# Cache rows, queries and new keys and values on SyncE's DMA queue instead of GpSimd's

## The chip, the cores and the metric

The kernel runs on one core of a Trainium2 chip. A core has five engines with an instruction stream each: TensorE (PE; its weight loads are listed apart as PEld), VectorE (DVE), ScalarE (ACT), GpSimd (POOL) and SyncE (SP). An engine that issues a DMA puts it on a queue of its own; 16 DMA engines move the bytes of all queues. The metric is the device time of one launch in microseconds, as the median of several runs.

## The reference

One layer of a decoder is computed for a prompt group (256 tokens) and a sample group (8 sequences of 4 new tokens with 1024 cached ones), all in float32. What matters here is its attention branch. There are three groups of 4 heads with 128 dimensions, and group (window, dilation) attends to every dilation-th key back to the window's end:

```python
DIL_GROUPS = ((128, 1), (512, 4), (2048, 16))
h = _rms_norm(x, g_pre_mix)
(qa, ka, va, za, ba, aa, qb, kb, vb, uc, ga, gb, gc) = _split(h @ w_in, IN_SPLITS)
...
def _dilated_group(q, k, v, q_idx, dil, n_back):
    dist = jnp.arange(n_back + 1) * dil
    idx = q_idx[:, None] - dist[None, :]
    ...
    kg = k[:, idx].astype(jnp.float32)
    vg = v[:, idx].astype(jnp.float32)
    s = jnp.einsum('bqhd,bqjhd->bqhj', q.astype(jnp.float32), kg) * (HD_B ** -0.5)
    s = jnp.where(valid[None, :, None, :], s, -jnp.inf)
    m = jnp.max(s, axis=-1)
    p = jnp.exp(s - m[..., None])
    return jnp.einsum('bqhj,bqjhd->bqhd', p, vg), m, jnp.sum(p, axis=-1)
...
    else:
        kv_all = [jnp.concatenate([win_hists[gi].astype(dt), kv_new[gi]], axis=1) for gi in range(N_GROUPS)]
        q_idxs = [kv.shape[1] - T + jnp.arange(T) for kv in kv_all]
        ob = _dilated_mixture([qb[:, :, gi] for gi in range(N_GROUPS)],
                              [kv[:, :, 0] for kv in kv_all], [kv[:, :, 1] for kv in kv_all], q_idxs)
    win_new = [kv_all[gi][:, -win:] for gi, (win, _) in enumerate(DIL_GROUPS)]
```

`_dilated_mixture` joins the three groups by their softmax denominators. Beside this branch there are a gated delta rule and a pooling branch, three gated projections that merge them, and a SwiGLU. Outputs are the activations and the new caches; the attention's caches (`win1` to `win3`, for prompt and sample) hold the new keys and values.

## The kernel before, in words

All 288 tokens (256 prompt, 32 sample) are worked on together, and what sets the time is the stream of weights: 585 tiles `raw` of 128 x 1024 float32 (512 KB), loaded by SyncE at L169 into five buffers. ScalarE casts each to `wh` (L180), VectorE takes the rest `wl` (L184), and TensorE does 24 matmuls with them (L253 to L255: high by high, low by high, high by low). Later a few more DMAs (L165) copy old cache rows to the outputs.

Beside this stream run background jobs, each a Python generator that emits its next instructions as tiles are taken, at so many a tile; `paced` ties these to the last `wl`, so that VectorE's order is tiles and background work interleaved. `attn_sample` is the one for the sample group, with 4.4 instructions of VectorE a tile (`R_S`). Its data:

- `nat`: the new queries, keys and values, transposed on TensorE (`knat`, L973) and brought to SBUF by ScalarE (L979) and VectorE (L981). From there the prompt's keys and values go to the output (`win_prompt`, L986, 128 KB each), and the sample's go to a DRAM scratch `scr` (L988, 32 KB) and to the output (`win_sample`, L991, 32 KB). `nat` shares its buffers (`U`) with other tensors, `oah` (L146) among them.
- `qt` and `big`: queries spread over partitions, from `scr` (L1089, L1095).
- `kr`: a cache row for 128 combinations, 128 x 512 float32 (256 KB), in five buffers (`KR`). A pass over keys (VectorE, L1142) and a pass over values (L1190, L1192) use 48 rows each of groups 2 and 3 (L1106), 8 each of group 1 (L1111), and a few from `scr` (L1089, L1112).

The sources of L1106 and L1111 differ in their leading indices. For L1106 it is four neighbouring cache rows, and then 32 combinations of sequence and query; for L1111 it is 128 combinations at once:

```python
for g, dil, n in ((1, 4, 32), (2, 16, 16)):
    src = cw[g].rearrange("b (q m r) k h d -> m k r (b q) (h d)", q=4, r=dil)
    ... dq.dma_start(kr, src[m, kv][:4])
src = cw[0].rearrange("b (s m) k h d -> m k (b s) (h d)", m=8)
    ... dq.dma_start(kr, src[m, kv])
```

A row four ahead is asked for before the row that VectorE works on next. A DMA in an engine's stream stands there until its buffer is free, and what the same engine issues later stands behind it. Prompt attention (`pv`, L1065, and `sc`, L1042 to L1057) runs on TensorE, ScalarE and VectorE in the same part of the program.

Of the kernel before, what the change touches and what calls it, by code (L numbers as in the profile page):

```python
# [17 lines left out]
NT, NP, NS = 288, 256, 32  # L18
# [6 lines left out]
KR = 5  # L25
EPS = 1e-6
SC = 128.0 ** -0.5
WIN = (128, 512, 1028)
# [60 lines left out]
class Layer:  # L89
# [865 lines left out]
    def evac_qkv(self, kind, g):  # L955
        vT = []

        def evac(h, ps):
            nc = self.nc
            t = self.res.popleft()  # L960
            nc.scalar.copy(t, ps)
            if kind == 2:
                vT.append(t)
            else:
                (self.kT if kind == 1 else self.qT)[g, h] = t
            if h < 3:
                return
            src = vT if kind == 2 else [(self.kT if kind == 1 else self.qT)[g, j] for j in range(4)]
            for tb in ([2] if kind == 0 else [1, 2] if (kind == 1 and g == 0) else [0, 1, 2]):
                w = NS if tb == 2 else 128  # L970
                p = self.ps("knat")
                for j in range(4):
                    nc.tensor.transpose(p[:w, j * 128:j * 128 + 128], src[j][:, tb * 128:tb * 128 + w],  # L973
                                        self.c["ident"])
                for hp in range(2):
                    n = self.U(name="nat")
                    cs = slice(hp * 256, hp * 256 + 256)
                    if hp == 0:
                        nc.scalar.copy(n[:w, :256], p[:w, cs])  # L979
                    else:  # L980
                        nc.vector.tensor_copy(n[:w, :256], p[:w, cs])  # L981
                    if tb < 2:
                        if not (g == 0 and tb == 0):
                            o = self.o[f"win{g + 1}_prompt"][0, 0].rearrange("r k h d -> r k (h d)")
                            r0 = 0 if g == 0 else tb * 128
                            self.dq.dma_start(o[r0:r0 + 128, kind - 1, cs], n[:, :256])  # L986
                    else:
                        self.dq.dma_start(self.scr[kind, g][:, cs], n[:NS, :256])  # L988
                        if kind > 0:
                            o = self.o[f"win{g + 1}_sample"][0].rearrange("b r k h d -> b r k (h d)")  # L990
                            self.dq.dma_start(o[:, WIN[g] - 4:, kind - 1, cs], n[:NS, :256])  # L991
                    if kind == 2 and tb < 2:
                        self.vn[g, tb, hp] = n
                    else:
                        self.free(n)
            self.free(*vT)
        evac.res = 4
        return evac
# [78 lines left out]
    def attn_sample(self, pool):  # L1077
        nc, c, a, scr = self.nc, self.c, self.a, self.scr
        dq = nc.gpsimd
        qt = pool.tile([128, 2, 512], F32, name="qt")  # L1080
        big = pool.tile([128, 4, 512], F32, name="big")
# [4 lines left out]
        def by_t(dst, kind, g):  # L1086
            src = scr[kind, g].rearrange("(b t) d -> t b d", t=4)
            for t in range(4):
                dq.dma_start(dst[t * 32:t * 32 + 32], src[t][:, None, :].to_broadcast([8, 4, 512]))  # L1089

        for g in (1, 2):
            by_t(qt[:, g - 1], 0, g)
        q0s = scr[0, 0].rearrange("(b t) d -> t b d", t=4)
        for t in range(4):
            dq.dma_start(big[:, t], q0s[t][:, None, :].to_broadcast([8, 16, 512]))  # L1095
        cw = [a["cache_win1"][0], a["cache_win2"][0], a["cache_win3"][0]]

        def row():
# [2 lines left out]
        def sources(kv):  # L1101

            for g, dil, n in ((1, 4, 32), (2, 16, 16)):
                src = cw[g].rearrange("b (q m r) k h d -> m k r (b q) (h d)", q=4, r=dil)
                for m in range(n):
                    yield g, (m if g == 1 else 32 + m), lambda kr, s=src[m, kv][:4]: dq.dma_start(kr, s)  # L1106
            for g in (1, 2):
                yield g, 47 + g, lambda kr, g=g: by_t(kr, 1 + kv, g)
            src = cw[0].rearrange("b (s m) k h d -> m k (b s) (h d)", m=8)
            for m in range(8):  # L1110
                yield 0, m, lambda kr, s=src[m, kv]: dq.dma_start(kr, s)  # L1111
            yield 0, 8, lambda kr: dq.dma_start(kr, scr[1 + kv, 0][:, None, :].to_broadcast([32, 4, 512]))  # L1112

        todo = deque((kv,) + r for kv in range(2) for r in sources(kv))
        got = deque()

        def load():
            kv, g, m, fill = todo.popleft()
            kr = row()
            fill(kr)  # L1120
            got.append((kv, g, m, kr))
# [7 lines left out]
                if not got:  # L1129
                    return  # L1130

        for _ in range(KR - 1):
            load()
        yield 5

# [44 lines left out]
        for g, m, kr in rows(1):  # L1180
            for h in range(4):
                hs = slice(h * 128, h * 128 + 128)
                for t in (range(4) if g == 0 else (0,)):
                    dst = o0[:, t, hs] if g == 0 else ot[:, hs]
# [336 lines left out]
```

## Time and profile before

| | |
|---|---|
| median of 3 runs | 2061.14 us (2057.72 to 2062.92) |
| the profiled execution | 2068.37 us, span 2066.6 us, mean granted clock 0.992 |
| busy | TensorE 2010.6, VectorE 1324.2, ScalarE 893.8, GpSimd 291.6 us |
| bytes on SyncE's queue (q1, hardware) | 384.72 MB |
| bytes on GpSimd's queue (q0, software) | 37.73 MB |
| keys' pass of `attn_sample` on VectorE | 452.3 to 742.9 us |
| values' pass | 775.9 to 1051.3 us |

Times are of one profiled execution. An engine's busy time is the sum of its instructions without waits. In a row of waits the engine and its instruction come first, then what it waited for, the sum in us, how often, and the longest; in a row of one line's DMAs stand count, issue time in ns (least, median, most) and the times of the first and the last. "Landing" is the time from a DMA's issue to its completion. The DMA share is the mean busy share of the 16 DMA engines, where an engine with packets of two queues at once counts for both.

### The profile page before, as it was taken

The page shows a single profiled execution, that of the slowest core. Times are in us where ns is not written, and L with a number is a line of the kernel's source. Part 1 is how long each engine was busy: PE and PEld are TensorE (multiplying, and loading weights), DVE is VectorE, ACT ScalarE, POOL GpSimd, SP SyncE. Part 2 cuts the span into 40 slices and gives each one's busy share as a digit, 9 for nine tenths or more (in the row PEclk, how much of TensorE's full clock was granted, in tenths as well). Part 3 has the DMA queues.
Part 4 walks back from the last instruction along what each step waited for, and adds up shares of the span by engine and source line. Part 5 has one row for each costly group of instructions (what it writes and reads, how often), then busy time and mean ns, then how long its engine had stood idle before and what let it go on. Part 6 is the DMA issues. An engine that isn't in the chain of part 4 may idle for free. (4 is left out here: it accounts for less than half of the span.)

```text
span 2066.6 us, 38707 instructions
## 1 busy us (share of the span) xinstructions
PE 2010.6 (97%) x15212; PEld 1984.4 (96%) x15212; DVE 1324.2 (64%) x2857; ACT 893.8 (43%) x1414; POOL 291.6 (14%) x504
## 2 busy tenths in 40 slices
PE   8999999999799999989999989999999999999998
PEld 8989998999799999989999989999999999999997
DVE  7969558567688779878875475543554445454555
ACT  6654473453344444333334454334333333333344
POOL 2326312523320022322000000000000000000001
PEclk9999999999999999999999989999999999999999
DMA  8565546959995668998677646766767767677662
GB/s 268 160 182 169 176 140 197 228 173 238 219 205 183 181 184 198 226 220 245 195 229 234 218 160 212 226 222 217 225 216 228 230 217 226 218 225 227 217 205 97
DMA packets 240310, 425.50 MB, mean 206 GB/s; under 512 B 42736, under 2 KB 83200, under 8 KB 238464
## 3 DMA queue, kind: packets, MB, share of 16 engines
q1 hardware_dynamic: 207712, 384.72, 63.1%
q0 software_dynamic: 32272, 37.73, 8.0%
q8 instruction: 119, 1.95, 0.4%
q10 hardware_dynamic: 144, 0.59, 0.1%
q14 instruction: 63, 0.52, 0.1%
HBM read 410.44 MB, written 66.63 MB: 231 GB/s over the span
## 5 line engine op out<-in xcount | busy, mean ns | idle before, releaser
L184 DVE TENSOR_TENSOR wl<-raw,wh 128x1024 fp32r<-128x1024 f32 x585 | 720.2, 1232 | 519.0 <-ACT wh L180 516.7
L180 ACT CAST wh<-raw 128x1024 fp32r<-128x1024 f32 x585 | 612.7, 1050 | 917.9 <-PE m L254 792.3
L253 PE MATMUL m<-hh,wh 128*128 128x288 f32 x1792 | 532.7, 299 | 4.2 <-ACT wh L180 3.7
L255 PE MATMUL m<-hh,wl 128*128 128x288 f32 x1792 | 524.0, 298 | 8.3 <-DVE wl L184 8.3
L254 PE MATMUL m<-hl,wh 128*128 128x288 f32 x1792 | 531.3, 298 | 0.0
L253 PE MATMUL m<-xgh,wh 128*128 128x288 f32 x1408 | 415.8, 297 | 4.0 <-ACT xgh L373 4.0
L254 PE MATMUL m<-xgl,wh 128*128 128x288 f32 x1408 | 415.8, 296 | 3.2 <-DVE xgl L374 3.2
L255 PE MATMUL m<-xgh,wl 128*128 128x288 f32 x1408 | 414.6, 296 | 0.0
L255 PEld LDWEIGHTS m<-hh,wl 128*128 128x128 f32 x1792 | 335.1, 189 | 13.1 <-DVE wl L184 10.7
L253 PEld LDWEIGHTS m<-hh,wh 128*128 128x128 f32 x1792 | 337.7, 189 | 7.8 <-ACT wh L180 4.2
L254 PEld LDWEIGHTS m<-hl,wh 128*128 128x128 f32 x1792 | 338.2, 189 | 1.9 <-issue 1.8
L253 PEld LDWEIGHTS m<-xgh,wh 128*128 128x128 f32 x1408 | 265.5, 189 | 4.6 <-ACT xgh L373 4.3
L254 PEld LDWEIGHTS m<-xgl,wh 128*128 128x128 f32 x1408 | 266.4, 189 | 3.6 <-DVE xgl L374 3.5
L255 PEld LDWEIGHTS m<-xgh,wl 128*128 128x128 f32 x1408 | 265.4, 189 | 0.0
L253 PE MATMUL m<-hidh,wh 128*128 128x288 f32 x704 | 207.5, 295 | 0.0
L254 PE MATMUL m<-hidl,wh 128*128 128x288 f32 x704 | 207.2, 295 | 0.0
L255 PE MATMUL m<-hidh,wl 128*128 128x288 f32 x704 | 206.5, 295 | 0.0
L1449 POOL TENSOR_TENSOR yo<-y,xr 128x288 f32<-128x288 f32 x7 | 5.6, 821 | 1060.7 <-DVE y L1440 1060.7
L254 PEld LDWEIGHTS m<-hidl,wh 128*128 128x128 f32 x704 | 132.4, 188 | 0.0
L253 PEld LDWEIGHTS m<-hidh,wh 128*128 128x128 f32 x704 | 132.2, 188 | 0.0
L255 PEld LDWEIGHTS m<-hidh,wl 128*128 128x128 f32 x704 | 131.9, 188 | 0.0
L1106 POOL DMA_DIRECT2D kr<-cache_win x96 | 65.4, 682 | 250.0 <-DVE junk L1142 136.9
(386 smaller groups left out, 2704.4 us busy)
## 6 DMA issues: line engine op xcount, KB each, us to landing
raw<-w_in SPq DMA_DIRECT2D x247, 512.0 KB, 4.5
raw<-w_gu SPq DMA_DIRECT2D x176, 512.0 KB, 4.0
raw<-w_down SPq DMA_DIRECT2D x88, 512.0 KB, 4.9
win_sample<-cache_win SPq DMA_DIRECT2D x64, 512.0 KB, 5.4
kr<-cache_win POOLq DMA_DIRECT2D x112, 256.0 KB, 10.7
raw<-w_out SPq DMA_DIRECT2D x32, 512.0 KB, 5.0
win_sample<-cache_win SPq DMA_DIRECT2D x32, 508.0 KB, 5.2
st<-state_gdn SPq DMA_DIRECT2D x64, 128.0 KB, 3.2
```

What stands on the lines that cost most here:

```text
L180: i = nc.scalar.copy(wh, raw)
L184: self.last_wl = nc.vector.tensor_tensor(wl, raw, wh.bitcast(F32), op=OP.subtract)
L253: nc.tensor.matmul(out, lhsT=wh[:, c], rhs=xh, start=k == 0, stop=False)
L254: nc.tensor.matmul(out, lhsT=wh[:, c], rhs=xl, start=False, stop=False)
L255: nc.tensor.matmul(out, lhsT=wl[:, c], rhs=xh, start=False, stop=k == nk - 1)
L1106: yield g, (m if g == 1 else 32 + m), lambda kr, s=src[m, kv][:4]: dq.dma_start(kr, s)
L1449: (nc.vector if how == "v" else nc.gpsimd).tensor_tensor(out[:, d % 2], y, x, op=OP.add)
```

## The change

The loads of `kr`, `qt` and `big` and the stores of `nat` are issued by SyncE (`nc.sync`) instead of GpSimd (`dq`), and the rows are asked for three ahead of the one to be worked instead of four; `kr` keeps its five buffers. GpSimd keeps the small transfers of the softmax (L1155 to L1167).

```diff
@@ the stores of nat
-                            self.dq.dma_start(o[r0:r0 + 128, kind - 1, cs], n[:, :256])
+                            nc.sync.dma_start(o[r0:r0 + 128, kind - 1, cs], n[:, :256])
...
-                        self.dq.dma_start(self.scr[kind, g][:, cs], n[:NS, :256])
+                        nc.sync.dma_start(self.scr[kind, g][:, cs], n[:NS, :256])
...
-                            self.dq.dma_start(o[:, WIN[g] - 4:, kind - 1, cs], n[:NS, :256])
+                            nc.sync.dma_start(o[:, WIN[g] - 4:, kind - 1, cs], n[:NS, :256])
@@ attn_sample: by_t (qt, and kr from scr), big
-                dq.dma_start(dst[t * 32:t * 32 + 32], src[t][:, None, :].to_broadcast([8, 4, 512]))
+                nc.sync.dma_start(dst[t * 32:t * 32 + 32], src[t][:, None, :].to_broadcast([8, 4, 512]))
...
-            dq.dma_start(big[:, t], q0s[t][:, None, :].to_broadcast([8, 16, 512]))
+            nc.sync.dma_start(big[:, t], q0s[t][:, None, :].to_broadcast([8, 16, 512]))
@@ attn_sample: the rows kr
-                    yield g, (m if g == 1 else 32 + m), lambda kr, s=src[m, kv][:4]: dq.dma_start(kr, s)
+                    yield g, (m if g == 1 else 32 + m), lambda kr, s=src[m, kv][:4]: nc.sync.dma_start(kr, s)
...
-                yield 0, m, lambda kr, s=src[m, kv]: dq.dma_start(kr, s)
+                yield 0, m, lambda kr, s=src[m, kv]: nc.sync.dma_start(kr, s)
-            yield 0, 8, lambda kr: dq.dma_start(kr, scr[1 + kv, 0][:, None, :].to_broadcast([32, 4, 512]))
+            yield 0, 8, lambda kr: nc.sync.dma_start(kr, scr[1 + kv, 0][:, None, :].to_broadcast([32, 4, 512]))
@@ attn_sample: the first rows
-        for _ in range(KR - 1):
+        for _ in range(KR - 2):
             load()
```

GpSimd's stream before, from the second store burst of the keys' pass to its third (a line of the kernel, the operation, the tile written and the one read, its shape, and how often in a row):

```order
L1106 DMA kr<-cache_win 128x1x512 x4
L986 DMA win_prompt<-nat_6164 128x256
L986 DMA win_prompt<-nat_6175 128x256
L986 DMA win_prompt<-nat_6167 128x256
L988 DMA scr<-nat_6186 32x256
L991 DMA win_sample<-nat_6186 8x4x256
L986 DMA win_prompt<-nat_6178 128x256
L988 DMA scr<-nat_6190 32x256
L991 DMA win_sample<-nat_6190 8x4x256
L1106 DMA kr<-cache_win 128x1x512 x8
```

The stores stand between rows there, so each store comes after the row ahead of it has got its buffer. In the changed kernel GpSimd's stream holds none of these any more.

SyncE's stream before, from shortly ahead of the same place to the end of the keys' pass:

```order
L169 DMA raw<-w_in 128x2x512 x47
L169 DMA raw<-w_br_a 128x2x512 x4
L169 DMA raw<-w_in 128x2x512 x8
L169 DMA raw<-w_br_a 128x2x512 x4
L169 DMA raw<-w_in 128x2x512 x3
L1229 DMA poolh<-poolh 128x480
```

SyncE's stream in the changed kernel, at the same store burst, with what each instruction waits for (`DMAHW0` to `DMAHW7` count the completions of SyncE's own DMAs, in turn; the others are the engines):

```order
L1106 DMA kr<-cache_win 128x1x512 [waits DMAHW2_49,DVE_49]
L986 DMA win_prompt<-nat_6162 128x256 [waits DMAHW3_49,Activation_49]
L986 DMA win_prompt<-nat_6165 128x256 [waits DMAHW4_49,DVE_49]
L986 DMA win_prompt<-nat_6173 128x256 [waits DMAHW5_49,Activation_49]
L986 DMA win_prompt<-nat_6176 128x256 [waits DMAHW6_49,DVE_49]
L988 DMA scr<-nat_6184 32x256 [waits DMAHW7_49,Activation_49]
L991 DMA win_sample<-nat_6184 8x4x256 [waits DMAHW0_49]
L988 DMA scr<-nat_6188 32x256 [waits DMAHW1_49,DVE_49]
L991 DMA win_sample<-nat_6188 8x4x256 [waits DMAHW2_49]
L1106 DMA kr<-cache_win 128x1x512 [waits DMAHW3_49,DVE_49]
L169 DMA raw<-w_in 128x2x512 [waits DMAHW4_49,Activation_49]
L169 DMA raw<-w_in 128x2x512 [waits DMAHW5_49,DVE_49]
```

Between raws stand now rows and, eight tiles apart, bursts of six or eight stores, and each DMA waits for the completion of the one eight places before it.

## The prediction

> **What bounds the kernel now.** I read the page's first lines, then what TensorE waited for, and then the stretches in which it waited.
>
> ```profile
> PE 2010.6 (97%) x15212; PEld 1984.4 (96%) x15212; DVE 1324.2 (64%) x2857; ACT 893.8 (43%) x1414; POOL 291.6 (14%) x504
> q1 hardware_dynamic: 207712, 384.72, 63.1%
> q0 software_dynamic: 32272, 37.73, 8.0%
> ```
> ```profile
> PE m L255 <- DVE wl L184: 14.7, 12, 2.8
> PE pv L1065 <- ACT pT L1057: 6.8, 1, 6.8
> ```
>
> TensorE is busy for 97% of the span, so whatever is gained by feeding it better comes out of the 56.0 us in which it idles. The two waits of 14.7 and 6.8 us fall mostly into two stretches, which are those in which most cache rows are loaded. The columns are length, busy time with instructions of TensorE, its weight loads, VectorE, ScalarE and GpSimd, granted clock, DMA share and GB/s.
>
> ```profile
> 455.00:600.00 145.00, 131.97 (x981) 130.00 (x979) 103.14 (x394) 59.81 (x92) 44.47 (x71) 0.98 0.98 217
> 800.00:940.00 140.00, 130.46 (x956) 128.32 (x956) 114.77 (x233) 50.88 (x62) 40.29 (x57) 0.99 1.05 221
> ```
>
> TensorE idles 13.0 us in the first and 9.5 us in the second: 22.5 us in all, the most that this change can win apart from a little clock (0.98 and 0.99). One cause is late rows: VectorE waits for them, and the weight splits `wl` queue behind it. The other is the stores: ScalarE's `oah` writes a buffer from which a store on GpSimd's queue, itself behind rows, has still to read.
>
> ```profile
> L1106 POOL DMA_DIRECT2D kr<-cache_win x96: 677/677/718, 392.0 to 932.7; - x96
>   DVE ot L1192: 21.8, 16
>   DVE junk L1142: 15.0, 8
> DMA to landing us min/median/max: 5.1/11.6/20.9
> ```
> ```profile
> ACT oah L146 <- DMA win_sample<-nat: 17.9, 2, 9.2
> ```
>
> **How a row travels.** This is what the forecast turns on. The 96 loads of L1106 have a source whose slowest index runs over four cache rows (`src[m, kv][:4]`); the 16 loads of L1111 also bring 256 KB, and their source's slowest index runs over 128.
>
> ```profile
> L1111 POOL DMA_DIRECT2D kr<-cache_win x16: 536/538/576, 618.3 to 984.8; - x16
> DMA to landing us min/median/max: 3.0/4.6/7.2
> ```
> ```profile
> 722.50:725.00 2.50, 2.50 (x22) 2.50 (x20) 2.11 (x4) 1.34 (x2) 0.00 (x0) 1.00 0.25 85
> 534.20:535.60 1.40, 0.96 (x7) 0.96 (x8) 1.30 (x8) 1.02 (x2) 0.39 (x1) 1.00 0.49 149
> 672.30:673.10 0.80, 0.80 (x8) 0.80 (x7) 0.80 (x5) 0.08 (x1) 0.00 (x0) 1.00 0.77 246
> ```
> ```profile
> q0 software_dynamic: 49, 0.20, 22.4%
> ```
>
> In 722.5 to 725.0 only one L1106 row moves (the last line is that stretch's queue), in 534.2 to 535.6 two, in 672.3 to 673.1 one row of L1111. The DMA share is 0.25, 0.49 and 0.77. So an L1106 row runs on four of the 16 engines, 64 KB on each, and two at a time run on eight: on GpSimd's queue the four move on from row to row. An L1111 row uses nearly all. One busy engine moves 0.20 MB / (0.224 x 16 x 2.5 us) = 22.3 GB/s.
>
> [...]
>
> **The change part by part.** *Removed from GpSimd:* 192 DMA issues of 0.5 to 0.7 us; that engine is 14% busy and bounds nothing, so I cost it at nothing.
>
> *Added to SyncE:* the same 192, and their bytes. The tiles, rows and stores of the two stretches:
>
> ```profile
> DMA packets 21430, 31.44 MB, mean 217 GB/s; under 512 B 9199, under 2 KB 9199, under 8 KB 21416
> L169 SPq DMA_DIRECT2D raw<-w_in x33: 367/368/368, 454.6 to 596.9; - x33
> L169 SPq DMA_DIRECT2D raw<-w_br_a x4: 367/368/368, 557.0 to 573.5; - x4
> DMA to landing us min/median/max: 4.3/9.8/14.0
> kr<-cache_win POOLq DMA_DIRECT2D x41, 256.0 KB, 9.9
> win_prompt<-nat POOLq DMA_DIRECT2D x14, 128.0 KB, 9.2
> scr<-nat POOLq DMA_DIRECT2D x8, 32.0 KB, 8.0
> win_sample<-nat POOLq DMA_DIRECT2D x8, 32.0 KB, 6.9
> ```
> ```profile
> L169 SPq DMA_DIRECT2D raw<-w_in x25: 367/368/368, 808.7 to 937.7; - x25
> L169 SPq DMA_DIRECT2D raw<-w_br_c x15: 367/368/368, 799.8 to 934.7; - x15
> L1106 POOL DMA_DIRECT2D kr<-cache_win x39: 677/677/698, 802.6 to 932.7; - x39
> DMA to landing us min/median/max: 7.9/13.0/18.0
> ```
>
> An issue costs SyncE 0.37 us. In the first stretch it would issue 37 + 41 + 30 = 108 DMAs, 40 us of 145. That is hidden: SyncE has nothing else to do.
>
> *Which engines the rows use on SyncE's queue.* The trace doesn't show it: no row there gives a SyncE transfer on fewer than all engines. The bounds are the four moving on, as on GpSimd's queue, and the same four for every row. I take the same four. A transfer on all 16 has no start to remember, so nothing in the kernel before needed one on this queue; GpSimd's queue is the nearer row but a different one, and it keeps the other bound a fair chance.
>
> [...]
>
> *The four engines' work.* Every tile puts 512/16 = 32 KB on each engine. In the first stretch each of the four carries 37 x 32 KB + 41 x 64 KB, plus about 0.16 MB of stores (14 x 8 KB, 8 x 2 KB, 8 x 4 KB), 4.06 MB; in the second 40 x 32 KB + 39 x 64 KB plus 0.05 MB of rows from `scr`, 3.92 MB. At 22.3 GB/s that is 182.1 and 175.8 us. TensorE's own work there is 132.0 and 130.5 us. Raws are issued four tiles ahead, four times 24 matmuls of 131.97/981 us or 12.9 us, and of this 3.6 us goes to the landing in a quiet stretch and 1.05 us to the cast:
>
> ```profile
> L169 SPq DMA_DIRECT2D raw<-w_in x12: 367/368/413, 250.3 to 298.1; - x12
> DMA to landing us min/median/max: 3.5/3.6/5.0
> L180 ACT CAST wh<-raw 128x1024 fp32r<-128x1024 f32 x585 | 612.7, 1050 | 917.9 <-PE m L254 792.3
> ```
>
> About 8 us of each stretch's shortfall is thus covered. TensorE would lose 182.1 - 132.0 - 8 = 42.1 us in place of 13.0 (+29.1), and 175.8 - 130.5 - 8 = 37.3 in place of 9.5 (+27.8): +57 us.
>
> The rate is the uncertain price. Upward, L1106 at its least lands 2.1 us after L1111 at its least for 48 KB more on an engine: 23.4 GB/s, which gives +40. Downward, the crowded first stretch moves 217 GB/s at share 0.98, 13.8 GB/s for an engine, and the second 221 at 1.05, 13.2; that gives +291. I stay at 22.3, since its row is the nearest: four engines working and twelve mostly idle. For the range I go to 18, half way down, which gives +142. The sum is nothing at (4.06 + 3.92 MB) / (140.0 + 138.5 + 22.5 us) = 26.5 GB/s, and above nothing below that.
>
> [...]
>
> *The stores.* They leave the rows' queue, so the 17.9 us of ScalarE go, and with them the 6.8 us of `pv`; both lie in the 13.0 us that the sum replaces. In the built program they stand in bursts of six to eight ahead of raws and wait for `nat`; the 8 us cover that, and where rows have eaten these, each burst adds a few us at most.
>
> *Rows three ahead.* The next row takes a buffer free since the row before last, so SyncE seldom stands at a row's wait with raws behind it: nothing. If the cover goes, a raw waits at most one row's VectorE work, 4 instructions.
>
> *Queries and `big`* (12 loads) stand in a stretch where raws land in 3.6 us: nothing.
>
> *Sum:* the profiled execution took 2068.4 us, its span 2066.6; +57 makes 2125. It lies 7 us above the median, 2061.1, so the forecast is 2118 us.
>
> **The rivals.** *Faster: the four move on.* Then each engine carries 31.4 MB / 16 = 1.97 MB in the first stretch, 88 us of 145, and no engine is the limit; ScalarE's hold goes and rows no longer queue behind stores. For it: 0.49 with two rows. Against a full win: share and landings there are already those of a crowded memory path, whoever issues. Of 22.5 us I give it 14: 2047. It decides wherever an L1106 transfer's share is found on changing engines.
>
> *No change.* Rows and raws land in 9.8 to 13 us because of the bytes in flight, 217 to 221 GB/s, which stay; the stores' gain is lost to bursts ahead of raws. 2061.
>
> *Slower by SyncE's order alone.* Each SyncE DMA also waits until the one eight places before has landed. With 78 rows and raws for 37 tiles, eight cover 3.8 tiles, 14.9 us at 3.9 us a tile; in the second stretch 14.2. Medians of 9.8 and 13.0 fit, the longest, 18.0, doesn't. Where it does not, raws slip by up to 4 us; three or four times makes 2071 to 2077.
>
> **How the numbers follow.** The same four engines: 0.62, own range 2090 to 2205 (from a little below +40 to +142). Four that move on: 0.20, at 2047. No change: 0.10. SyncE's order: 0.08. About 0.02 of the first falls within 0.3% (6 us, about what can be told from no change), where the rate is near 26.5. Slower 0.68, same 0.12, faster 0.20. The cases of both signs make a wide range: 2045 to 2205 leaves out the better half of the fast case and the rates below 18 GB/s, together about 2 in 10.
>
> **What would show it.** Right: in the two stretches, lengthened to some 170 us each, TensorE is busy for about three quarters, waiting for `wh` and `wl`, and behind these ScalarE for raws; raw and row landings reach 12 to 18 us while the DMA share falls to about 0.5, since twelve engines idle. A stretch with a row in flight and no raw shows share 0.25, and never 0.5 with two. ScalarE's wait for `win_sample` is gone, the software queue's 37.7 MB shrink to almost nothing. Wrong: raws land in 5 us among rows, or the share stays near 1.0 with TensorE at over 95%: then rows use changing engines. If TensorE waits while a raw's landing is short but its issue late, it is SyncE's order.

## The result and the profile after

The changed kernel takes 2144.34 us (median of 4 runs, 2140.69 to 2145.19), the kernel before 2062.03 us beside it: a ratio of 1.0398, with a 95% interval of 1.0376 to 1.042. It is 82 us slower, where 57 were forecast. The profiled execution has a span of 2143.4 us and a granted clock of 0.98. The ratios of the experiments below are likewise to the kernel before as it ran beside them, with medians from 2063.66 to 2067.07 us.

The page's engines and queues, in the form shown of before:

```profile
PE 2029.8 (95%) x15212; PEld 1996.9 (93%) x15212; DVE 1325.1 (62%) x2857; ACT 892.3 (42%) x1414; POOL 159.6 (7%) x312
q1 hardware_dynamic: 228704, 420.83, 63.8%
q0 software_dynamic: 1072, 1.45, 0.3%
```

The rows and stores have moved to SyncE's queue: 37.73 MB became 1.45 MB on GpSimd's. TensorE now idles 2143.4 - 2029.8 = 113.6 us in place of 56.0, and its same 15212 matmuls are busy for 19.2 us longer. The span's +76.8 us is these two, +57.6 and +19.2. (The two profiled executions lie 76.8 us apart and the medians 82: that of before was 6.3 us above its median, that of after 0.9.)

What TensorE waited for longest, and below it ScalarE's and VectorE's waits behind these (sum, times, longest):

```profile
PE m L255 <- DVE wl L184: 42.5, 30, 5.3
PE pv L1065 <- ACT pT L1057: 12.1, 2, 11.9
PE m L253 <- ACT wh L180: 9.9, 1, 9.9
...
PE av L812 <- DVE y L807: 5.6, 1, 5.6
```
```profile
ACT wh L180 <- DMA raw<-w_in: 84.2, 28, 9.3
...
ACT oah L146 <- DMA win_sample<-nat: 30.6, 2, 16.8
```
```profile
DVE ot L1192 <- DMA kr<-cache_win: 46.1, 29, 4.3
DVE junk L1142 <- DMA kr<-cache_win: 46.0, 25, 3.1
```

VectorE's waits for rows have grown from 36.8 us to 92.1, and ScalarE's for the raws of `w_in` from 22.0 us to 84.2. The two stretches with most rows (length, TensorE, weight loads, VectorE, ScalarE, GpSimd, clock, DMA share, GB/s):

```profile
455.00:655.00 200.00, 162.84 (x1160) 158.77 (x1159) 121.25 (x455) 68.45 (x106) 0.00 (x0) 0.91 0.59 176
855.00:1050.00 195.00, 162.05 (x1115) 156.17 (x1114) 134.28 (x268) 55.43 (x67) 13.86 (x16) 0.93 0.61 187
```

TensorE stands still for 37.2 and 33.0 us in them, while the DMA engines move less, not more: 176 and 187 GB/s where before it was 217 and 221, at a share of 0.59 and 0.61 in place of 0.98 and 1.05. Something other than the total of bytes holds them. Two short windows out of the first stretch, 0.7 us apart, show what:

```profile
572.00:574.20 2.20, 2.20 (x17) 2.20 (x17) 2.06 (x8) 1.05 (x1) 0.00 (x0) 0.93 0.26 99
574.90:576.40 1.50, 1.50 (x14) 1.50 (x13) 0.00 (x0) 0.35 (x1) 0.00 (x0) 1.00 0.91 300
```

In the first, as much is busy as four engines of 16 (0.26); then nearly all work (0.91), as a raw on all of them would have it. SyncE's own stream at this place (start, time to issue, what is issued):

```profile
568.17 2.95 SPq L1106 DMA_DIRECT2D kr<-cache_win  x2
571.21 2.47 SPq L169 DMA_DIRECT2D raw<-w_in  x1
573.77 1.21 SPq L1106 DMA_DIRECT2D kr<-cache_win  x1
575.07 2.85 SPq L169 DMA_DIRECT2D raw<-w_in  x1
578.01 1.25 SPq L1106 DMA_DIRECT2D kr<-cache_win  x1
579.36 1.43 SPq L169 DMA_DIRECT2D raw<-w_in  x1
580.88 4.01 SPq L1106 DMA_DIRECT2D kr<-cache_win  x1
584.98 2.43 SPq L169 DMA_DIRECT2D raw<-w_in  x1
587.51 1.26 SPq L1106 DMA_DIRECT2D kr<-cache_win  x1
588.86 3.22 SPq L169 DMA_DIRECT2D raw<-w_in  x1
592.18 1.26 SPq L1106 DMA_DIRECT2D kr<-cache_win  x1
```

Two rows had been issued ahead of the first window and a raw was being issued in it, and still no more than four engines' worth was busy. A raw's issue, 0.37 us at the median before, takes 1.43 to 3.22 us here, where a row is ahead of it, and 4.26 us at the longest of `w_in` (4.77 us of `w_br_c`):

```profile
L169 SPq DMA_DIRECT2D raw<-w_in x247: 363/368/4258, 3.1 to 1113.4; - x124
```

From 573.77 to 592.18 us SyncE issues four rows and four raws, one in 4.60 us, and is busy issuing for 17.7 of the 18.4 us. If each of four engines carries 64 KB of a row and 32 KB of a raw in 4.60 us, it moves 21.4 GB/s.

### The profile page after: what moved, and what is told of

The parts are those of the page before. It is cut to its first block, busy times and chain, and to the rows that moved or that the text cites. A ratio compares the mean times of both kernels' runs of the same rounds, so it can differ in the third digit from the quotient of the medians.

```text
span 2143.4 us, 38670 instructions
## 1 busy us (share of the span) xinstructions
PE 2029.8 (95%) x15212; PEld 1996.9 (93%) x15212; DVE 1325.1 (62%) x2857; ACT 892.3 (42%) x1414; POOL 159.6 (7%) x312
## 3 DMA queue, kind: packets, MB, share of 16 engines
q0 software_dynamic: 1072, 1.45, 0.3%
## 5 line engine op out<-in xcount | busy, mean ns | idle before, releaser
L255 PEld LDWEIGHTS m<-hidh,wl 128*128 128x128 f32 x704 | 132.0, 188 | 0.0
L1192 DVE SCALAR_TENSOR_TENSOR ot<-kr,sct,ot 128x128 f32<-128x128 f32 x196 | 70.6, 360 | 50.3 <-DMA kr<-cache_win 46.1
L1142 DVE SCALAR_TENSOR_TENSOR junk<-kr,qt 128x128 f32<-128x128 f32 x200 | 58.2, 291 | 51.1 <-DMA kr<-cache_win 46.0
```

What stands on the lines that cost most here:

```text
L255: nc.tensor.matmul(out, lhsT=wl[:, c], rhs=xh, start=False, stop=k == nk - 1)
L1142: self.paced(nc.vector.scalar_tensor_tensor(junk, kr[:, hs], SC, q, op0=OP.mult, op1=OP.mult, accum_out=out))
L1192: self.paced(e.scalar_tensor_tensor(dst, kr[:, hs], pr, dst, op0=OP.mult, op1=OP.add))
```

## The experiments

Theory A is the prediction's: an L1106 row, whose source's slowest index has four entries, runs on four engines, and on SyncE's queue always on the same four, which then hold up every raw. The rivals: B, SyncE's order of issue (one queue, stores and rows ahead of raws, eight places); B', the store bursts alone; C, the queue as such; D, the number of rows ahead; E, the address steps of the rows.

**Sixteen engines on SyncE's queue.**

```diff
-                    yield g, (m if g == 1 else 32 + m), lambda kr, s=src[m, kv][:4]: nc.sync.dma_start(kr, s)
+                    yield g, (m if g == 1 else 32 + m), lambda kr, s=src[m, kv][:4]: nc.sync.dma_start(kr, s.rearrange("r c d -> c r d"))
...
-                nc.sync.dma_start(dst[t * 32:t * 32 + 32], src[t][:, None, :].to_broadcast([8, 4, 512]))
+                nc.sync.dma_start(dst[t::4], src[t][:, None, :].to_broadcast([8, 4, 512]))
...
-    d["sel1"] = (t // 32 == c % 4) & ((t % 32) // 4 == c // 4)
+    d["sel1"] = (t % 4 == c % 4) & (t // 16 == c // 4)
```

Beside these, the mask `maskt` follows the new order of partitions, and two small transfers of the softmax become four each.

> The changed kernel, with one thing altered: each of the 96 loads of L1106 has the 32 combinations of sequence and query as its source's slowest index and the four cache rows inside, so that partition p stands for query-combination p // 4 and token p % 4 (queries, masks, fold matrices and two softmax transfers follow that order; the transfers become 4 instead of 1). Bytes, queue, issue order and lead stay. Theory A (the rows' 64 KB lie on the same four of the 16 engines): rows are now spread over 16 engines, an engine carries about 2 MB instead of 4 in each crowded stretch, the loss goes, and the time is 2035 to 2062 us; L1106 issues take 0.4 us like a tile's instead of 1.2. Rival B (SyncE's order: one queue, stores and rows ahead of raws, eight places): nothing in that changed, 2135 to 2150 us.

Measured: 2034.64 us, ratio to before 0.9842 (0.9827 to 0.9856). The edit turns a loss of 4.0% into a gain of 1.6%. The page and the row of L1106's issues, and the two stretches of before:

```profile
PE 2001.4 (98%) x15212; PEld 1979.3 (97%) x15212; DVE 1327.9 (65%) x2857; ACT 894.5 (44%) x1414; POOL 174.8 (9%) x318
```
```profile
L1106 SPq DMA_DIRECT2D kr<-cache_win x96: 534/546/703, 393.3 to 899.5; - x96
```
```profile
455.00:600.00 145.00, 145.00 (x1107) 144.49 (x1106) 119.97 (x453) 67.02 (x102) 0.00 (x0) 1.00 0.77 246
800.00:940.00 140.00, 140.00 (x1061) 140.00 (x1060) 126.91 (x253) 50.46 (x56) 13.86 (x16) 1.00 0.78 244
```

TensorE doesn't idle there at all. Queue, order and bytes are the changed kernel's, so rival B isn't the cause. The issue takes 0.55 us at the median (0.4 was expected) in place of 1.20:

```profile
L1106 SPq DMA_DIRECT2D kr<-cache_win x96: 528/1196/4009, 393.5 to 1006.9; - x96
```

which is the row of the changed kernel. Its long issues thus come with the four engines, and are no price of SyncE's queue as such.

**Eight and two engines.** Two doses of the same thing.

```diff
-                src = cw[g].rearrange("b (q m r) k h d -> m k r (b q) (h d)", q=4, r=dil)
+                src = cw[g].rearrange("b (n r) k h d -> r k b n (h d)", n=32)
...
-                    yield g, (m if g == 1 else 32 + m), lambda kr, s=src[m, kv][:4]: nc.sync.dma_start(kr, s)
+                    yield g, (m if g == 1 else 32 + m), lambda kr, s=src[m % 16, kv][:, :16]: nc.sync.dma_start(kr, s)
```

> The changed kernel, with the loads of L1106 reading other cache rows of the same sizes (8 sequences x 16 rows, 128 pieces of 2 KB), so that the slowest index has 8 entries; the sample's attention therefore works on other rows than the reference's. Theory A: eight engines with 32 KB each. Their load in both stretches is 2.7 + 2.6 MB, at 20.8 GB/s (the rate that gives the measured +82) 257 us, less than TensorE's 262: no loss, 2035 to 2070 us. Rival B: 2135 to 2150.

```diff
-                src = cw[g].rearrange("b (q m r) k h d -> m k r (b q) (h d)", q=4, r=dil)
+                src = cw[g].rearrange("b (n r) k h d -> r k (b n) (h d)", n=8)
...
-                    yield g, (m if g == 1 else 32 + m), lambda kr, s=src[m, kv][:4]: nc.sync.dma_start(kr, s)
+                    yield g, (m if g == 1 else 32 + m), lambda kr, s=src[m]: nc.sync.dma_start(kr, s)
```

> The changed kernel, with the loads of L1106 reading the key and the value of 64 other cache rows (128 pieces of 2 KB), so that the slowest index has 2 entries; the sample's attention works on other data than the reference's. Theory A: two engines with 128 KB each, 6.75 + 6.47 MB in the two stretches, at 20.8 GB/s 635 us against 278.5 of work and cover and 22.5 already lost: +334, 2340 to 2450 us. Rival B: 2135 to 2150.

Measured: 2058.67 us with eight, ratio 0.9961 (0.9949 to 0.9974); 2363.12 us with two, ratio 1.143 (1.1413 to 1.1447). With the changed kernel's four entries and the 32 of the first experiment, the time falls as the slowest index gets more of them: ratios of 1.143, 1.0398, 0.9961 and 0.9842 for 2, 4, 8 and 32. That two and four entries are two and four engines is read from shares of 0.13 (below) and 0.26; eight and 16 engines for 8 and 32 entries are the theory's, and no share of such a row alone was read. The two-engine kernel in its two stretches, and in 6 us of the first:

```profile
455.00:770.00 315.00, 205.68 (x1275) 196.97 (x1274) 128.54 (x480) 78.62 (x131) 1.98 (x4) 0.80 0.38 120
900.00:1220.00 320.00, 224.00 (x1346) 215.65 (x1344) 152.52 (x326) 73.14 (x95) 27.89 (x51) 0.81 0.40 124
714.00:720.00 6.00, 6.00 (x45) 6.00 (x44) 2.71 (x10) 2.60 (x3) 0.00 (x0) 0.90 0.13 49
```

The DMA share has fallen to 0.38, in the 6 us to 0.13 (two engines of 16), and TensorE is busy for two thirds. The estimate of +334 went by 20.8 GB/s; measured is about +296, close to the +292 that the prediction's own 22.3 GB/s gives for two engines. In the profiled execution it is +295.0, of which +213.0 is idle time of TensorE and +82.0 longer busy time; the clock is down to 0.80 there.

**The stores back on GpSimd's queue, rows on SyncE's.** One of the three stores; the other two likewise.

```diff
-                            nc.sync.dma_start(o[r0:r0 + 128, kind - 1, cs], n[:, :256])
+                            self.dq.dma_start(o[r0:r0 + 128, kind - 1, cs], n[:, :256])
```

> The changed kernel with the stores of nat back on GpSimd's queue; rows and queries stay on SyncE's. Theory A: the stores carry 4% of the four engines' bytes and are not the cause: 2125 to 2145 us. Rival B': the store bursts ahead of raws (SyncE waits for nat there) make a good part of the loss: 2080 to 2110.

Measured: 2142.14 us, ratio 1.0363 (1.0347 to 1.0378). The changed kernel has 1.0398 (1.0376 to 1.042). The intervals just overlap; by the ratios 7 of the 82 us would come from the stores. B' as the main cause falls.

**Only the stores on SyncE's queue.** Rows and queries as before; again one store of three.

```diff
-                            self.dq.dma_start(o[r0:r0 + 128, kind - 1, cs], n[:, :256])
+                            nc.sync.dma_start(o[r0:r0 + 128, kind - 1, cs], n[:, :256])
```

> The kernel before with only the stores of nat on SyncE's queue; rows and queries stay on GpSimd's. Theory A: the stores spread over 8 or 16 engines, cost SyncE's queue nothing that shows, and free ScalarE's oah: between 2050 and 2064 us, pv's 6.8 us smaller. Rival B' (bursts of stores ahead of raws hold SyncE): 2066 to 2085 us.

Measured: 2066.57 us, ratio 1.0014 (0.9997 to 1.0031), that is no change. Theory A's gain didn't come; in microseconds the time lies just inside the rival's 2066 to 2085, but the kernel before took 2063.66 beside it, so the rival's loss isn't there either. ScalarE's wait and TensorE's for `pT`:

```profile
ACT oah L146 <- DMA scr<-nat: 18.8, 2, 10.5
```
```profile
PE pv L1065 <- ACT pT L1057: 3.5, 1, 3.5
```

`pv`'s wait is smaller, as expected. But `oah` still waits 18.8 us for stores, after 17.9 before. The stores land late here too: L986's take 11.2 us at the median (of the eleven whose landing the trace has), 7.9 before. With rows over 16 engines on SyncE's queue that wait is 2.2 us:

```profile
ACT oah L146 <- DMA win_sample<-nat: 2.2, 2, 1.9
```

With rows over 16 engines on GpSimd's queue, the stores behind them (the first kernel of the next experiment), `oah` waits for no store (for 1.6 us when it ran again), and L986's land in 3.0 us. So it is not the queue alone that makes stores late. Nor is it the rows' four engines alone: with rows on SyncE's queue and stores on GpSimd's (the experiment above) `oah` waits for no store either, and L986's land in 5.4 us. What decides between these cases is not shown.

**Sixteen engines on GpSimd's queue.** The kernel before with the new order of partitions, first with the stores there, then with the stores on SyncE's queue.

```diff
-                    yield g, (m if g == 1 else 32 + m), lambda kr, s=src[m, kv][:4]: dq.dma_start(kr, s)
+                    yield g, (m if g == 1 else 32 + m), lambda kr, s=src[m, kv][:4]: dq.dma_start(kr, s.rearrange("r c d -> c r d"))
```

> The kernel before, with the same new order of partitions: L1106 has a slowest index of 32 and runs on 16 engines, still on GpSimd's queue, with the stores there and four rows ahead. Theory A (a row's four engines are the trouble on either queue, less where they move on): late rows and raws go, TensorE's 22.5 us of idle time in the two stretches fall to under 10, 2035 to 2052 us. Rival C (GpSimd's queue itself, its issue and its stores behind rows, costs the time; the pattern matters on SyncE's queue alone): 2055 to 2068 us.

> Rows on GpSimd's queue over 16 engines, stores of nat on SyncE's. Theory A: as good as rows and stores both on SyncE's queue over 16 engines (2035 us), within 8 us: the queue as such is worth little once no engine is crowded. Rival C (the queue matters): 10 to 25 us above it.

Measured: 2040.03 us, ratio 0.9875 (0.9847 to 0.9903), and 2038.38 us, ratio 0.9867 (0.984 to 0.9895). Four engines to a row were thus the trouble in the kernel before as well. The first of these in the two stretches of before:

```profile
455.00:600.00 145.00, 145.00 (x1106) 144.49 (x1105) 120.10 (x455) 66.13 (x101) 42.54 (x79) 1.00 0.80 247
800.00:940.00 140.00, 140.00 (x1060) 140.00 (x1059) 127.38 (x253) 50.46 (x56) 39.61 (x64) 1.00 0.78 243
```

Its landings of L1106, which were 5.1, 11.6 and 20.9 us before, and the raws' from 455 to 600 us, which were 4.3, 9.8 and 14.0:

```profile
DMA to landing us min/median/max: 2.8/4.0/9.5
```
```profile
DMA to landing us min/median/max: 3.4/4.4/6.4
```

The same 256 KB land in a third of the time, and the raws among them in less than half.

**Four rows ahead instead of three,** with 16 engines on SyncE's queue.

```diff
-        for _ in range(KR - 2):
+        for _ in range(KR - 1):
             load()
```

> Rows over 16 engines on SyncE's queue, as in the 2035 us kernel, but asked for four ahead instead of three. The prediction's step (three ahead costs and brings nothing that shows): 2031 to 2040 us. Rival D (four ahead makes SyncE stand at a row's buffer with raws behind it): 2040 to 2060 us, with TensorE waiting for raws again.

Measured: 2036.43 us, ratio 0.9858 (0.9829 to 0.9886), beside 0.9842 (0.9827 to 0.9856) with three: no difference, as the prediction's step had it, and rival D falls. This is shown for rows over 16 engines only.

**The address steps.** The new order of partitions also changes the order of a row's addresses, so the slowest index was kept at four entries and the addresses changed.

```diff
-                src = cw[g].rearrange("b (q m r) k h d -> m k r (b q) (h d)", q=4, r=dil)
+                src = cw[g].rearrange("b r k h d -> k b r (h d)")
...
-                    yield g, (m if g == 1 else 32 + m), lambda kr, s=src[m, kv][:4]: nc.sync.dma_start(kr, s)
+                    yield g, (m if g == 1 else 32 + m), lambda kr, s=src[kv][0:4, m % 8 * 32:m % 8 * 32 + 32]: nc.sync.dma_start(kr, s)
```

> The changed kernel, with L1106 reading 4 sequences x 32 neighbouring cache rows (pieces of 2 KB 4 KB apart, instead of 512 KB or 1 MB apart): the slowest index keeps 4 entries; the sample's attention works on other rows than the reference's. Theory A (four engines): 2130 to 2150 us as before the edit. Rival E (the wide address steps of the 32 pieces that an engine reads in a row make the rows slow): 2035 to 2080 us.

> The kernel before with the same reads, on GpSimd's queue with its moving four engines. Theory A (four engines at a time are the trouble there too): 2055 to 2068 us. Rival E (the address steps, which rows16 changed as well, are what made rows and raws land late): 2035 to 2048 us.

Measured: 2149.57 us, ratio 1.0413 (1.0393 to 1.0434), on SyncE's queue, and 2067.42 us, ratio 1.0013 (1.0 to 1.0027), on GpSimd's. Neither moves from its counterpart with wide steps, and rival E falls on both queues.

**The queue by itself,** once no engine is crowded: the two 16-engine kernels of above again, unedited, on one chip.

> The kernel with rows over 16 engines, rows and stores on SyncE's queue, again, on one chip with its counterpart on GpSimd's queue (next run). If the queue is worth nothing: the two ratios within 0.2% of each other. If SyncE's queue is worth what the first runs leave possible: this one lower by 3 to 9 us.

> The counterpart: rows over 16 engines, rows and stores on GpSimd's queue. Expected 2036 to 2042 us, 0 to 9 us above the run before.

Measured: 2035.88 us (2034.62 to 2038.72), ratio 0.9867 (0.9847 to 0.9886), on SyncE's; 2040.74 us (2039.13 to 2042.25), ratio 0.9888 (0.9871 to 0.9905), on GpSimd's. The ratios' intervals overlap, the runs don't: some 5 us in favour of SyncE's queue. TensorE in the stretch of `attn_sample`, of the one and then of the other:

```profile
400.00:1100.00 700.00, 697.53 (x5287) 692.66 (x5286) 559.59 (x1530) 301.72 (x443) 40.67 (x73) 1.00 0.70 219
```
```profile
400.00:1100.00 700.00, 697.52 (x5287) 692.65 (x5286) 559.11 (x1530) 301.74 (x444) 132.00 (x242) 1.00 0.70 219
```

It is the same to 0.01 us, so the difference doesn't arise there. It arises behind the last instruction that works, where GpSimd's stream ends with a `DRAIN` (the longest of three in these rows, of the one and then of the other):

```profile
L1519 POOLq DRAIN  x3: 40/98/3772, 2028.4 to 2033.8; - x3
L1519 POOLq DRAIN  x3: 51/98/9574, 2027.2 to 2037.3; - x3
```

It takes 3.8 us of the one and 9.6 us of the other, where SyncE's stream is done at 2032.0 us and the program waits for GpSimd. Up to this `DRAIN` the kernel with rows on GpSimd's queue is 1.2 us ahead (2027.2 against 2028.4). Why it takes longer is open: in the kernel before, with rows on GpSimd's queue too, it takes 4.0 us.

## Why the prediction was right, and where its sizes were off

*The same four engines.* Right. The window with share 0.26, with several rows issued, shows four engines where GpSimd's queue had eight at work with two rows (0.49); and the ratio falls from 1.143 to 0.9842 as the slowest index goes from 2 entries to 32. Which four of the 16 they are, no run here shows.

*The rate.* Right: 22.3 GB/s was taken, and 21.4 is read from SyncE's stream and 99 GB/s / (0.26 x 16) = 23.8 from the short window with four engines.

*The two stretches.* Right in size. They have to be compared by their work, since the same work takes longer after: by ScalarE's casts `wh`, the same 37 tiles of the first and the 40 of the second lie in these windows, before and then after:

```profile
455.50:601.30 145.80, 132.77 (x986) 130.80 (x985) 103.98 (x398) 59.78 (x92) 44.21 (x71) 0.98 0.99 218
800.10:940.80 140.70, 131.16 (x962) 129.02 (x961) 115.43 (x234) 50.84 (x62) 40.72 (x58) 0.99 1.05 221
```
```profile
463.80:640.90 177.10, 139.94 (x987) 136.10 (x985) 102.75 (x395) 59.09 (x92) 0.00 (x0) 0.90 0.59 176
844.20:1013.80 169.60, 141.79 (x985) 136.26 (x983) 114.56 (x232) 50.60 (x62) 10.73 (x12) 0.95 0.61 181
```

They became 31.3 and 28.9 us longer, where the prediction's sum had 29.1 and 27.8.

*TensorE's own work* was taken as fixed, 132.0 and 130.5 us, and nothing was put down for the clock. In these windows the granted clock fell from 0.98 and 0.99 to 0.90 and 0.95, and TensorE was busy for 139.9 and 141.8 us; so it idled for 37.2 and 27.8 us and not for the 42.1 and 37.3 forecast. That step was wrong, but it didn't move the sum, in which own work cancels: 182.1 - 8 - 145 is +29.1 whatever part of it TensorE works. With two engines it is the same: the sum had +292 in all, and 82.0 of the +295.0 are busy time.

*An issue of 0.37 us, hidden.* Wrong in size. In the changed kernel SyncE is busy issuing for nearly all of the time among rows (17.7 of 18.4 us above), and by this it is at their issue that a row holds up the raws behind it. The prediction had named late issues as the sign of SyncE's order; they are there, and it took the kernel with 16 engines, in the same order, to tell the two apart.

*What the sum left out.* The rest of the profile's +76.8 us lies outside the two stretches, where the sum had nothing: again by tiles, +8.5 between 392 and 455 us, +4.2 behind the first stretch and +5.3 behind the second (less 1.4 elsewhere). This, more than the 3.3 us by which the sum was short in the stretches, is what makes 57 too small; that TensorE's idle time grew by 57.6 us, the very figure forecast, is luck. The +4.2 and +5.3 were not traced further. The +8.5 come from the first rows. Queries and `big`, which the prediction put at nothing, cost nothing: with 16 engines, where the queries bring the same bytes in the new order of partitions, TensorE is busy for all 35.00 us from 395 to 430 us. But where the first five rows are issued, SyncE stands for 11 us, the raws behind them are late, and TensorE idles for 5.6 us (`av` in the waits above) and is busy for 2.9 us longer at a clock of 0.95:

```profile
393.48 11.18 SPq L1106 DMA_DIRECT2D kr<-cache_win  x5
404.76 10.08 SPq L169 DMA_DIRECT2D raw<-w_in  x5
```
```profile
ACT wh L180 <- DMA raw<-w_in: 9.3, 1, 9.3
```

(the second fence is ScalarE's wait from 395 to 425 us).

*The stores.* The prediction let ScalarE's 17.9 us and `pv`'s 6.8 us go. They grew to 30.6 and 12.1; since the sum replaced the whole idle time, this didn't move it, but the step was wrong: in the kernel with only the stores moved they land late on SyncE's queue as well (L986's in 11.2 us at the median). What a store, or a row from `scr`, puts on each of the four engines, 0.16 and 0.05 MB in the sum (by an estimate 7 and 2 us at 22.3 GB/s), no run shows; with the stores back on GpSimd's queue some 7 us of the 82 went, by ratios whose intervals just overlap.

*The signs.* The stretches were to be some 170 us long with TensorE busy for three quarters and a share of about 0.5; they are 177.1 and 169.6 us, 79% and 84%, 0.59 and 0.61. Landings of 12 to 18 us can't be read: the changed kernel's trace has none of SyncE's DMAs.

*The rivals.* "Faster" was wrongly argued: it set the late landings down to a crowded memory path "whoever issues", and gave 14 of the 22.5 us. With the same bytes over 16 engines all 22.5 us go on either queue; on GpSimd's the share in the first stretch falls from 0.98 to 0.80 while the rate rises from 217 to 247 GB/s. "No change" and "SyncE's order alone" fell with the 16-engine kernel.

## What to carry to other kernels

Before a transfer is moved to another queue, look at the slowest index of its source and at the DMA share while it moves alone: a share of a quarter (0.25 before, 0.26 after) was four engines here, and on SyncE's queue, where the rows kept to the same four, these became the bound of everything behind them (a ratio of 1.0398). Putting an index with 32 entries outermost, here by another order of partitions, was worth more than any choice of queue: ratios of 0.9875 on GpSimd's and 0.9842 on SyncE's to the kernel before. A forecast should also look at the places outside the most crowded stretches, here where the first rows are issued; and it should compare stretches by their work. The clock, down to 0.90 and 0.95 in the two stretches here, needed no term of its own, since the four engines set their length.

## What the runs showed of the hardware that was not expected

- Issuing a DMA on SyncE's queue took longer among rows on four engines: a raw 0.37 us at the median before, up to 4.77 us in the changed kernel; a row there 1.20 us at the median, and 2.2 us each for five in a row. With rows over 16 engines a row's issue took 0.55 us.
- With rows on four engines that move on, raws landed late: 9.8 us at the median among rows, against 4.4 us when the same bytes went over 16. Why is not shown.
- The granted clock fell to 0.80 where TensorE was busy for two thirds of the time (two engines), and to 0.91 at 81% (four).
- With rows over 16 engines, GpSimd's closing `DRAIN` took 9.6 us with the rows on GpSimd's queue and 3.8 us with them on SyncE's, and the program waited for it.
